# Turning chunks of a ConvFFN's input later and loading operands of its down projection earlier, in a one-layer decoder kernel on one core

## The chip, the core and the metric

The kernel runs on one core of one Trainium2 chip. The metric is device time in microseconds (us). The kernel before took 2790.61 us in the median of three runs (2783.90 to 2791.97); one further execution was profiled.

The engines are named as in the profile: PE is TensorE (matrix products and transposes), DVE is VectorE, ACT is ScalarE, POOL is GpSimd. SP is the engine from which nearly all DMA transfers of this kernel are issued.

## The reference

One layer of a decoder, for a prompt of 2048 tokens (with 16 meta tokens in front) and for 8 sequences that each get one new token over 4096 cached ones. Token mixing is half stick-breaking attention, half pooling over trailing windows. What matters here is the channel mixer behind it, a gated feed-forward with a causal depthwise convolution of width 3:

```python
def conv_ffn(h, prefix, w_up, conv_w, conv_b, w_down):
    up = h @ w_up
    L = up.shape[1]
    ext = jnp.concatenate([prefix.astype(up.dtype), up], axis=1)
    c = conv_b + sum(conv_w[i] * ext[:, i:i + L] for i in range(CONV_W))
    gate, val = c[..., :D_FF], c[..., D_FF:]
    out = (jax.nn.silu(gate) * val) @ w_down
    return out, ext[:, L + 2 - (CONV_W - 1):]
...
        h2 = rmsnorm(xp, norm_ffn_g)
        f, conv_prompt = conv_ffn(h2, zero_prefix, w_up, conv_w, conv_b, w_down)
        xp = xp + f
    y_prompt = rmsnorm(xp, norm_final_g)[:, N_META:]
```

D_MODEL is 1024 and D_FF 2816, so w_up is 1024 x 5632 and w_down 2816 x 1024. All data is float32.

## The kernel before

**Products.** Every float32 operand is split into a high part (a cast to fp32r, on ACT, line 159) and a low part (the difference, on DVE, line 160). A product is three matmuls (lines 165 to 167): high by high, high by low, low by high. The matmuls of 128 x 128 by 128 x 512 accumulate in a PSUM tile of 128 x 512, one bank.

**Stages.** The projection of the input, attention and the mixer's output come first. This document is about the two stages that follow.

The **up projection** runs over 2048 tokens in four chunks of 512 columns (`h2c`, CW = 512) and over 22 pairs of weight tiles (gate and value, NF = 22), in 44 steps `it` (line 998). The steps 0 to 21 take chunks 0 and 1, the steps 22 to 43 take chunks 2 and 3, with all weights loaded a second time. A step loads the next pair of weight tiles (`load_up`, tiles `uwr`, `uwh`, `uwl`, pool `puw` with three buffers of each), and then, for each of its two chunks and for gate and value, makes 24 matmuls into one bank (`psu`), evicts them with the convolution on ACT and DVE (lines 1032 to 1042, tile `cv`), multiplies on POOL and stores the result to `act_s` in DRAM (line 1048).

A chunk stands in DRAM as rows (`h2_s`) and has to be turned: four tiles of 128 rows are loaded (`xn`), each is transposed on PE in two halves of four 128 x 128 blocks (`tp` for chunks 0 and 1, line 794; `tp3c` for chunks 2 and 3, line 821), and each half is split into its place in `h2c`. These halves use the same six PSUM banks as the products (`psu`, pool `pu_mm`). Chunks 0 and 1 are turned by `h2_first` before the first product; the `xn` tiles of `h2_first` borrow buffers of `uwr`, `uwh` and `uwl`. Chunk 2 is turned at the head of steps 4 and 5, two tiles (16 transposes) each; chunk 3 is turned after the last product of step 21, four tiles in a row. It takes the place of chunk 0 (pool `pha`), chunk 2 has a third place (`phb`). Tiles for chunks 2 and 3 have two buffers, so the third tile is loaded when the first is turned (line 823).

Within the up projection the decode of the 8 sequences runs beside the products: gathers on POOL, sums on DVE (lines 876 and 878), values on PE (`dav`, line 946). It ends in step 42, where its memory is released (`dec.close()`, line 1005).

The **down projection** runs over 16 tiles of 128 rows, twice: half `hf` 0 takes the first 11 of the 22 tiles of w_down and adds to the residual, half 1 takes the other 11 and normalises. For a row tile `load_act` loads `ar` (704 KB) and splits it into `ah` and `al`; two halves of 512 columns are then accumulated in `psd`, 33 matmuls each. At the end of the up projection the kernel has loaded the operand of row tile 0 (in step 42, pool `pdx`) and w_down tiles 0 to 2 (in step 43, pool `puw`). Tiles 3 to 10 are loaded at the head of the stage (tile `wd`, pool `pdw`, ten buffers); all pass through the three `uwr` buffers. Row tiles alternate between the pools `pdx` and `pd`, one operand each.

Beside this, ten "few" rows (8 samples and 2 prompt rows) go through the output projection, the up and the down projection in small products (`fewd`, `few`) whose weights come in as `raw` tiles of 512 KB, four buffers. `FSTEP` sets how many of their 42 steps have been emitted before a row tile. The first four `raw` loads, `gfin` (the last gain) and the residual rows `xs` are emitted at the head of the stage, and `conv_states` before row tile 3.

**What sets the order.** The program's order is not the order of each engine: a scheduler that simulates a timeline at build time reorders the instructions within what dependencies and buffers allow. The order on each engine, SP's queue among them, is then fixed in the program.

Of the kernel before, what the change touches and what calls it, by code (L numbers as in the profile page):

```python
# [1 line left out]

# [6 lines left out]
F32 = mybir.dt.float32  # L9
# [9 lines left out]
P = 128  # L19
D = 1024  # L20
NK = D // P
# [23 lines left out]
RAWB = 4  # L45
FSTEP = lambda i: 3 * i // 2
# [14 lines left out]
def hymba_kernel(  # L61
# [710 lines left out]

    def load_act(pool, hf, a0, n):
        ar = pool.tile([P, HF, P], F32, name="ar", bufs=1)
        nc.sync.dma_start(out=ar[:, :, :n], in_=act_s[hf * HF:(hf + 1) * HF, :, a0:a0 + n].rearrange("f p n -> p f n"))
        ah = pool.tile([P, HF, P], F32R, name="ah", bufs=1)
        al = pool.tile([P, HF, P], F32R, name="al", bufs=1)
        split(ah[:, :, :n], al[:, :, :n], ar[:, :, :n])
        return ah, al

    with ExitStack() as es:
        phb = es.enter_context(tc.tile_pool(name="h2b", bufs=2, reuse_waits="tile"))

        def h2_first(ch):

            h2c[ch] = (phb if ch else pha).tile([P, 2, NK, CW], F32R, name="h2c")
            for a in range(4):
                i = 1 + 4 * ch + a
                xn = puw.tile([P, NK, P], F32, name="xn0", tag=("uwr", "uwh", "uwl")[(a + ch) % 3]).rearrange("p c n -> p (c n)")
# [11 lines left out]
        h2_first(1)  # L801
# [11 lines left out]
        def h2_turn(ch, a):  # L813

            if a == 0:
                h2c[ch] = (pha if ch == 3 else phb).tile([P, 2, NK, CW], F32R, name="h2c")
            xn = h2x.pop((ch, a))
            for c4 in range(0, NK, 4):
                tp = psm.tile([P, 4, P], F32, name="tp3c", tag="psu")
                for c in range(4):  # L820
                    nc.tensor.transpose(tp[:, c, :], xn[:, (c4 + c) * P:(c4 + c + 1) * P], ident)
                split(h2c[ch][:, 0, c4:c4 + 4, a * P:(a + 1) * P], h2c[ch][:, 1, c4:c4 + 4, a * P:(a + 1) * P], tp)
            if a < 2:
                h2_load(ch, a + 2)
# [173 lines left out]
        for it in range(2 * NF):  # L998
            half, f = divmod(it, NF)
            ws = ws_next  # L1000
            if it + 1 < 2 * NF:
                ws_next = [load_up((it + 1) % NF), load_up(NF + (it + 1) % NF)]
            if it == 2 * NF - 2:
# [15 lines left out]
            for k in (2 * half, 2 * half + 1):  # L1019
                if 2 * it + k % 2 == 2:  # L1020
# [28 lines left out]
            if it == NF - 1:  # L1049
                for a in range(4):  # L1050
                    h2_turn(3, a)
# [4 lines left out]
    with ExitStack() as es:  # L1056
        pdw = es.enter_context(tc.tile_pool(name="pdw", bufs=HF - 1, side="right", reuse_waits="tile"))
# [20 lines left out]
        nc.sync.dma_start(out=gfin, in_=norm_final_g.partition_broadcast(P))  # L1078
# [91 lines left out]
        nc.sync.dma_start(out=xs[0:NS, :], in_=x_sample)  # L1170
        nc.sync.dma_start(out=xs[NS:NSO, :], in_=meta_tokens[META - 2:META, :])
# [9 lines left out]

        for t in range(RAWB):
            load_raw(t)
        raw_at[0] = RAWB
        dt_ = [(P * i, P, NS + META + P * i) for i in range(16)]
        for hf in range(2):
            wd = []
            for c in range(HF):
                f = hf * HF + c
                if f < 3:  # L1190
                    wd.append(wd_first[c])
                else:
                    wd.append(load_down(f, puw if hf == 1 and 2 <= c < 5 else pdw))
            for ti, (a0, n, xc) in enumerate(dt_):
                if (hf, ti) == (0, 3):
                    conv_states()
                few_to(FSTEP(16 * hf + ti))
                ah, al = act_first if (hf, ti) == (0, 0) else load_act((pdx, pd)[(hf * len(dt_) + ti) % 2], hf, a0, n)
# [40 lines left out]
```

## Time and profile before

| | |
|---|---|
| median of three runs | 2790.61 us (2783.90 to 2791.97) |
| the profiled execution, its own time | 2794.02 us |
| its span, first to last instruction | 2792.3 us |
| mean granted TensorE clock | 0.984 |
| first product of the up projection | 1174.68 us after the start of the span |
| first product of the down projection | 2238.59 us |
| last product of the down projection | 2782.48 us |

How to read the lines in the prediction. A row of the waits has the engine and line that waited, what ended the wait, and then the total in us, the number of times and the longest. A row of the timeline has its start, its length in us, the engine, the line and operation, output and inputs, and in brackets the idle time of the engine ahead of it and what ended that. A row of the stretches has its bounds, its length, the busy time of PE with the number of matmuls (or of all five engines, PE, its weight loads, DVE, ACT and POOL), the granted clock, the share of the DMA engines and GB/s. A row of groups has the line, engine, operation, count, then busy time in total and the mean of one in ns; a row of one tile has the least, median and largest duration in ns. Matmuls overlap: one is shown with 0.39 us, but the next starts 0.23 us after it.

### The profile page before, as it was taken

What the parts mean: (1) busy time and instruction counts of PE and PEld (TensorE: products, weight loads), DVE (VectorE), ACT (ScalarE), POOL (GpSimd) and SP (SyncE); (2) the same over time, 40 slices, a digit from 0 to 9 for tenths busy, and PEclk for the clock granted to TensorE, in tenths of its full rate; (3) what the DMA queues carried; (4) which work ended last, traced back from release to release, by engine and by line L of the source; (5) the groups of instructions that cost most, each with busy time, mean ns of one, the idle gap of its engine ahead of it and who ended that gap; (6) DMA issues with size and microseconds to landing.
All of it is one profiled execution on the core that took longest, in us unless ns stands there. A gap on an engine that the chain in (4) does not pass through costs nothing.

```text
span 2792.3 us, 39757 instructions
## 1 busy us (share of the span) xinstructions
PE 2670.0 (96%) x14759; PEld 2097.0 (75%) x14759; DVE 1805.2 (65%) x3037; ACT 1034.1 (37%) x1833; POOL 718.9 (26%) x736
## 2 busy tenths in 40 slices
PE   5899999999998999899999999999999989999998
PEld 4677877777786888687877777777776767777777
DVE  4588768866769688668977776877774442114434
ACT  4466656655556356323322222222222221002111
POOL 0012112211122011135555554545553200000000
PEclk9899999999999999999999999999999999999999
DMA  7653542464426432545556555646656484666551
GB/s 249 220 186 104 188 162 90 130 212 135 158 91 190 148 109 96 185 162 189 167 207 246 209 199 212 216 177 234 205 216 238 138 282 151 207 202 216 178 177 64
DMA packets 326376, 498.79 MB, mean 179 GB/s; under 512 B 25368, under 2 KB 238632, under 8 KB 309782
## 3 DMA queue, kind: packets, MB, share of 16 engines
q1 hardware_dynamic: 307749, 362.03, 39.5%
q0 software_dynamic: 18432, 134.23, 12.6%
q8 instruction: 116, 1.90, 0.3%
q14 instruction: 79, 0.64, 0.1%
HBM read 395.99 MB, written 100.59 MB: 178 GB/s over the span
## 4 chain that ended last, share of the span: by engine, by line
PE 78%; DVE 3%; DMA 3%; issue 2%; ACT 1%; POOL 0%; SPq 0%; DVEq 0%; ACTq 0%; POOLq 0%
PE psu L165 11%; PE psu L166 11%; PE psu L167 11%; PE psd L165 6%; PE psd L167 5%; PE psd L166 5%; PE po L614 4%; PE z L517 3%; PE tt L571 3%; PE psm L165 2%; PE psm L167 2%; PE psm L166 2%; PE dav L946 2%; PE pso L165 2%; PE pso L167 2%; PE pso L166 2%
## 5 line engine op out<-in xcount | busy, mean ns | idle before, releaser
L165 PE MATMUL psu<-h2c,uwh 128*128 128x512 f32 x1408 | 554.0, 393 | 4.9 <-DVE h2c L160 4.9
L166 PE MATMUL psu<-h2c,uwh 128*128 128x512 f32 x1408 | 551.2, 391 | 0.0
L167 PE MATMUL psu<-h2c,uwl 128*128 128x512 f32 x1408 | 550.3, 391 | 0.0
L533 POOL TENSOR_TENSOR be<-be,om 128x512 f32<-128x512 f32 (+3 forms) x176 | 184.0, 1045 | 841.1 <-DVE om L528 273.8
L1035 DVE SCALAR_TENSOR_TENSOR cv<-psu,par,cv 128x511 f32<-128x511 f32 x352 | 261.2, 742 | 163.8 <-ACT cv L1032 162.1
L165 PEld LDWEIGHTS psu<-h2c,uwh 128*128 128x128 f32 x1408 | 265.3, 188 | 81.2 <-issue 10.3
L1046 POOL TENSOR_TENSOR cv<-cv,cv 128x512 f32<-128x512 f32 x88 | 216.7, 2462 | 373.4 <-DVE cv L1040 285.7
L166 PEld LDWEIGHTS psu<-h2c,uwh 128*128 128x128 f32 x1408 | 265.2, 188 | 62.2 <-issue 8.5
L167 PEld LDWEIGHTS psu<-h2c,uwl 128*128 128x128 f32 x1408 | 265.0, 188 | 61.9 <-issue 7.3
L528 DVE TENSOR_TENSOR_SCAN om<-om,zero 128x513 f32<-128x513 f32 (+1 forms) x224 | 273.2, 1223 | 45.0 <-ACT om L518 40.0
L518 ACT ACTIVATE om<-z,nbias 128x512 f32<-128x512 f32 (+5 forms) x360 | 213.7, 595 | 137.3 <-PE z L517 85.7
L1032 ACT ACTIVATE cv<-psu,par 128x512 f32<-128x512 f32 x176 | 136.6, 776 | 298.2 <-PE psu L167 298.2
L1206 DVE TENSOR_TENSOR xt<-psd,xt 128x512 f32<-128x512 f32 x64 | 44.0, 691 | 285.3 <-PE psd L167 280.5
L519 ACT ACTIVATE be<-z,bias 128x512 f32<-128x512 f32 (+5 forms) x360 | 211.8, 591 | 0.6 <-PE tt L571 0.6
L166 PE MATMUL psm<-hk,wh 128*128 128x512 f32 x512 | 207.4, 405 | 2.9 <-DVE hk L225 2.9
L165 PE MATMUL psm<-hk,wh 128*128 128x512 f32 x512 | 205.9, 408 | 2.0 <-ACT hk L224 1.7
L167 PE MATMUL psm<-hk,wl 128*128 128x512 f32 x512 | 205.3, 401 | 1.1 <-DVE wl L160 1.0
L166 PE MATMUL psd<-wd,ah 128*128 128x512 f32 x512 | 200.8, 393 | 2.9 <-DVE wd L160 2.9
L160 DVE TENSOR_TENSOR uwl<-uwr,uwh 128x1024 fp32r<-128x1024 f32 x94 | 123.5, 1316 | 122.1 <-ACT uwh L159 118.7
L165 PE MATMUL psd<-wd,ah 128*128 128x512 f32 x512 | 201.5, 398 | 0.8 <-ACT wd L159 0.8
L167 PE MATMUL psd<-wd,al 128*128 128x512 f32 x512 | 201.2, 394 | 0.0
L159 ACT CAST uwh<-uwr 128x1024 fp32r<-128x1024 f32 x94 | 98.8, 1053 | 236.7 <-PE psu L166 224.9
(245 smaller groups left out, 4782.9 us busy)
## 6 DMA issues: line engine op xcount, KB each, us to landing
hk<-hs_s SPq DMA_DIRECT2D x96, 512.0 KB
uwr<-in_w_up_dram SPq DMA_DIRECT2D x88, 512.0 KB
act_s<-sg SPq DMA_DIRECT2D x88, 256.0 KB
ar<-act_s SPq DMA_DIRECT2D x32, 704.0 KB
raw<-in_w_up_dram SPq DMA_DIRECT2D x40, 512.0 KB
xt<-in_x_prompt_dram SPq DMA_DIRECT2D x32, 512.0 KB
hs_s<-hk SPq DMA_DIRECT2D x32, 512.0 KB
uwr<-in_w_down_dram SPq DMA_DIRECT2D x22, 512.0 KB
```

Of the source, the lines that this page charges most:

```text
L160: nc.vector.tensor_tensor(out=lo, in0=src, in1=f32(hi), op=ALU.subtract)
L165: nc.tensor.matmul(ps, ah, bh, start=i == 0, stop=False)
L166: nc.tensor.matmul(ps, ah, bl, start=False, stop=False)
L167: nc.tensor.matmul(ps, al, bh, start=False, stop=i == n - 1)
L518: nc.scalar.activation(out=om[:M, e, 0:n], in_=z[:M, :n], func=AF.Sigmoid, scale=-SCALE, bias=nbias[:M, h:h + 1])
L519: nc.scalar.activation(out=be[:M, e, 0:n], in_=z[:M, :n], func=AF.Sigmoid, scale=SCALE, bias=bias[:M, h:h + 1])
L528: nc.vector.tensor_tensor_scan(out=rv, data0=rv, data1=zero[:M, 0:1].broadcast_to([M, n + 1]), initial=st["prev"][:M, e, 0:1], op0=ALU.mul ...
L533: (nc.gpsimd if cnt["mul"] % 2 == 0 else nc.vector).tensor_tensor(out=be[:M, e, m0:n], in0=be[:M, e, m0:n], in1=om[:M, e, m0 + 1:n + 1], o ...
L614: mm = nc.tensor.matmul(o, v_, a_, start=start, stop=stop, skip_group_check=True).ins
L1032: nc.scalar.activation(out=t, in_=ps, func=AF.Identity, scale=cpar(2, fi), bias=cpar(3, fi))
L1035: nc.vector.scalar_tensor_tensor(out=t[:, o:], in0=ps[:, 0:CW - o], scalar=cpar(d, fi), in1=t[:, o:], op0=ALU.mult, op1=ALU.add)
L1046: nc.gpsimd.tensor_tensor(out=cv[1], in0=cv[0], in1=cv[1], op=ALU.mult)
```

## The change

- `h2_first(1)`, the turn of chunk 1, moves from before the first product to step 0, between its products on chunk 0 and those on chunk 1. The load of the weights for step 1 moves behind it. The tiles of chunk 1 borrow other buffers.
- `h2_turn` now turns half a tile. For chunk 2 one half tile is turned before each of the eight chunk passes of steps 4 to 7. For chunk 3 all eight half tiles are turned in step 21 before its pass over chunk 1, as soon as chunk 0 has been used for the last time.
- In step 42 three w_down tiles (3 to 5) are loaded into a new pool `pde` of three buffers; in step 43 the operand of row tile 1 is loaded as well. `load_act` now has two sets of buffers in `pdx`, used in turn for all row tiles. `pdw` has seven buffers, and tiles 5 to 7 of half 1 take those of `pde`.
- The first loads for the few rows move from the head of the stage to row tile 1, `gfin` to row tile 3, and the few rows' steps one row tile later (`FSTEP`).

```diff
-FSTEP = lambda i: 3 * i // 2
+RAWB, WDE = 4, 3
+FSTEP = lambda i: 3 * max(i - 1, 0) // 2
...
     def load_act(pool, hf, a0, n):
-        ar = pool.tile([P, HF, P], F32, name="ar", bufs=1)
+        i = next(act_no) % 2
+        ar = pool.tile([P, HF, P], F32, name=f"ar{i}", bufs=1)
...
         h2_first(0)
         ws_first = [load_up(0), load_up(NF)]
-        h2_first(1)
...
-            if it + 1 < 2 * NF:
+            if 0 < it < 2 * NF - 1:
                 ws_next = [load_up((it + 1) % NF), load_up(NF + (it + 1) % NF)]
             if it == 2 * NF - 2:
...
-                act_first = load_act(pdx, 0, 0, P)
+                pde = ctx.enter_context(tc.tile_pool(name="pde", bufs=WDE, side="right", reuse_waits="tile"))
+                act_first = [load_act(pdx, 0, 0, P)]
+                wd_early = [load_down(3 + c, pde) for c in range(WDE)]
             if it == 2 * NF - 1:
                 wd_first = [load_down(c, puw) for c in range(3)]
+                act_first.append(load_act(pdx, 0, P, P))
...
-            if it in (4, 5):
-                h2_turn(2, 2 * it - 8)
-                h2_turn(2, 2 * it - 7)
...
             for k in (2 * half, 2 * half + 1):
+                if (it, k) == (0, 1):
+                    h2_first(1)
+                    ws_next = [load_up(1), load_up(NF + 1)]
+                if 4 <= it < 8:
+                    h2_turn(2, it - 4, 4 * k)
+                if (it, k) == (NF - 1, 1):
+                    for a in range(4):
+                        for c4 in (0, 4):
+                            h2_turn(3, a, c4)
...
-            if it == NF - 1:
-                for a in range(4):
-                    h2_turn(3, a)
...
-        pdw = es.enter_context(tc.tile_pool(name="pdw", bufs=HF - 1, side="right", reuse_waits="tile"))
+        pdw = es.enter_context(tc.tile_pool(name="pdw", bufs=HF - 1 - WDE, side="right", reuse_waits="tile"))
...
             for ti, (a0, n, xc) in enumerate(dt_):
+                if (hf, ti) == (0, 1):
+                    few_begin()
                 if (hf, ti) == (0, 3):
                     conv_states()
+                    nc.sync.dma_start(out=gfin, in_=norm_final_g.partition_broadcast(P))
```

Where instructions now stand, at three places. First DVE at the start of the up projection, behind the split of the second weight tile and the clearing of `zdec`: `h2c<-tp` are the low parts of chunk 1's half tiles, `cv` the evictions of products, `uwl` a weight tile. Before:

```order
L976 MEMSET zdec 128x2048
L853 TENSOR_SCALAR seg<-seg 128x8
L160 TENSOR_TENSOR h2c<-tp_12760,h2c 128x4x128
L160 TENSOR_TENSOR h2c<-tp_12767,h2c 128x4x128
L931 TENSOR_REDUCE rsel<-hsel 128x4
L933 TENSOR_REDUCE msel<-hsel 128x8
L160 TENSOR_TENSOR h2c<-tp_12776,h2c 128x4x128
L160 TENSOR_TENSOR h2c<-tp_12783,h2c 128x4x128
```

and in the change:

```order
L1048 SCALAR_TENSOR_TENSOR cv_12865<-psu,par,cv_12865 128x511
L161 TENSOR_TENSOR h2c<-tp_12878,h2c 128x4x128
L161 TENSOR_TENSOR h2c<-tp_12885,h2c 128x4x128
L1048 SCALAR_TENSOR_TENSOR cv_12865<-psu,par,cv_12865 128x510
L1055 COPY carry<-psu 128x2
L161 TENSOR_TENSOR uwl<-uwr,uwh 128x1024
L161 TENSOR_TENSOR h2c<-tp_12894,h2c 128x4x128
L858 TENSOR_SCALAR pt_12764<-pt_12764 128x8
L161 TENSOR_TENSOR h2c<-tp_12901,h2c 128x4x128
L161 TENSOR_TENSOR h2c<-tp_12910,h2c 128x4x128
L161 TENSOR_TENSOR h2c<-tp_12917,h2c 128x4x128
```

The half tiles of chunk 1 stood ahead of every eviction and now stand among those of the value product on chunk 0, with a weight tile between them.

Second PE at the turn of chunk 3: `tp3c` are the transposes of a tile, `dav` a step of the decode, `psu` the products. Before:

```order
L821 MATMUL tp3c<-ident,xn_16408 128x128 x8
L821 MATMUL tp3c<-ident,xn_16410 128x128 x8
L946 MATMUL dav<-kvd,zdec 32x512 x8
L821 MATMUL tp3c<-ident,xn_16577 128x128 x8
L821 MATMUL tp3c<-ident,xn_16593 128x128 x8
L165 MATMUL psu<-h2c,uwh 128x512
```

and in the change:

```order
L823 MATMUL tp3c<-ident,xn_16408 128x128 x8
L823 MATMUL tp3c<-ident,xn_16410 128x128 x8
L950 MATMUL dav<-kvd,zdec 32x512 x8
L823 MATMUL tp3c<-ident,xn_16504 128x128 x8
L823 MATMUL tp3c<-ident,xn_16520 128x128 x8
L166 MATMUL psu<-h2c,uwh 128x512
```

The group has moved by 48 matmuls as a whole, and nothing stands between its tiles that did not before.

Third SP's queue at the head of the down projection, from the first of the row tiles' residual loads (`xt`): `uwr` is a tile of w_down, `raw` a tile for the few rows. Before:

```order
L757 DMA uwr<-in_w_down_dram 128x1024
L1078 DMA gfin<-in_norm_final_g_dram 128x1024
L1200 DMA xt_20450<-xp_s 128x1024
L775 DMA ar<-act_s 128x11x128
L1200 DMA xt_20538<-xp_s 128x1024
L1200 DMA xt_20633<-xp_s 128x1024
L757 DMA uwr<-in_w_down_dram 128x1024
L1113 DMA gf<-in_norm_ffn_g_dram 10x1024
L1092 DMA raw<-wf_s 128x1024 x4
```

and in the change:

```order
L1101 DMA raw<-in_w_out_dram 128x1024 x2
L1214 DMA xt_20531<-xp_s 128x1024
L1214 DMA xt_20619<-xp_s 128x1024
L1210 DMA gfin<-in_norm_final_g_dram 128x1024
L1122 DMA gf<-in_norm_ffn_g_dram 10x1024
L1061 DMA act_s<-sg 128x512
L1101 DMA raw<-wf_s 128x1024 x3
L758 DMA uwr<-in_w_down_dram 128x1024
L1077 DMA out_dram<-co 88x128
L1101 DMA raw<-wf_s 128x1024
L758 DMA uwr<-in_w_down_dram 128x1024 x2
```

The operand `ar` is no longer there (four of them now stand further ahead), the loads of `w_out` for the few rows have come in, and the `uwr` loads of w_down tiles 9 and 10 stand behind and between those of `wf_s`.

More of the change, by code (lines that the diff above doesn't have):

```diff
@@ L1 @@
 from contextlib import ExitStack
+from itertools import count
 import concourse.bass as bass
@@ L788, in h2_first @@
                 i = 1 + 4 * ch + a
-                xn = puw.tile([P, NK, P], F32, name="xn0", tag=("uwr", "uwh", "uwl")[(a + ch) % 3]).rearrange("p c n -> p (c n)")
+                xn = puw.tile([P, NK, P], F32, name="xn0", tag=(("uwr", "uwh", "uwl", "uwr"), ("uwh", "uwl", "uwr", "uwr"))[ch][a]).rearrange("p c n -> p (c n)")
                 nc.sync.dma_start(out=xn, in_=h2_s[TILES[i][0]:TILES[i][0] + P, :])
```

47 lines of the change are left out of this document (24 added, 23 removed).

## The prediction

> **What bounds the kernel now.** I read the page first.
>
> ```profile
> PE 2670.0 (96%) x14759; PEld 2097.0 (75%) x14759; DVE 1805.2 (65%) x3037; ACT 1034.1 (37%) x1833; POOL 718.9 (26%) x736
> ```
>
> TensorE (PE) is busy for 2670.0 of the 2792.3 us of the span. Whatever is gained must come out of its idle time, or out of time in which it runs at a lower clock. So the next view is the waits of PE, of which these six rows lie where the change acts (us in total, times, longest):
>
> ```profile
> PE tp L794 <- DMA xn<-h_s: 12.6, 2, 10.6
> PE psu L165 <- DVE h2c L160: 4.9, 1, 4.9
> PE psd L165 <- ACT ah L159: 3.9, 1, 3.9
> PE tp3c L821 <- DMA xn<-h_s: 3.0, 2, 2.7
> PE psd L166 <- DVE wd L160: 2.9, 1, 2.9
> PE fewd L1102 <- DMA raw<-wf_s: 0.5, 2, 0.3
> ```
>
> They are four places: the turn of chunk 1 (tp), that of chunk 2 (psu behind h2c), that of chunk 3 (tp3c), and the start of the down projection (psd, fewd). The third view is the table by stretches for PE alone: length, PE busy (matmuls), granted clock, DMA share, GB/s.
>
> ```profile
> 1156.20:1174.60 18.40, 5.80 (x32) 0.69 0.77 239
> 1174.60:1176.93 2.33, 2.33 (x9) 0.51 0.27 72
> 1200.00:1260.00 60.00, 60.00 (x266) 1.00 0.35 119
> 1293.18:1296.34 3.16, 3.15 (x7) 0.50 1.04 432
> 1704.46:1705.90 1.44, 1.44 (x6) 0.50 0.96 406
> 2249.03:2252.13 3.10, 3.09 (x7) 0.51 1.02 377
> 2263.03:2269.15 6.12, 6.11 (x14) 0.50 0.85 298
> ```
>
> In the undisturbed stretch 266 matmuls take 60.00 us, 0.226 us each. Behind each wait the clock is at half for 1.44 to 6.12 us, which costs half of that time again: a wait costs more than its idle time. Between 1200 and 2240 us PE has no other gaps of size, so a microsecond won at one of these places is won at the end.
>
> **Chunk 1 behind the first products.** The timeline around the start of the up projection:
>
> ```profile
> 1154.83 1.40 PE L794 MATMUL tp<-ident,xn 128*128 128x128 f32 x8 [1.00 <-DVE h2c L160]
> 1159.28 1.21 DVE L160 TENSOR_TENSOR uwl<-uwr,uwh 128x1024 fp32r<-128x1024 f32 x1
> 1160.94 1.05 SPq L790 DMA_DIRECT2D xn<-h_s  x2
> 1162.58 1.23 DVE L160 TENSOR_TENSOR uwl<-uwr,uwh 128x1024 fp32r<-128x1024 f32 x1
> 1166.81 4.42 PE L794 MATMUL tp<-ident,xn 128*128 128x128 f32 x24 [10.58 <-DMA xn<-h_s]
> 1173.26 1.77 PE L794 MATMUL tp<-ident,xn 128*128 128x128 f32 x8 [2.02 <-DMA xn<-h_s]
> ```
>
> Chunk 0 is turned at 1156.2 us and the first weight tile is split at 1160.5 (1159.28 + 1.21), the second at 1163.8. PE nevertheless waits for the loads of chunk 1 and starts its products at 1174.6. The 96 products of the first step (48 for each of two chunks) last 96 x 0.226 = 21.7 us, plus 1.2 us for the half clock: they end at 1197.5.
>
> In the change the 48 products on chunk 0 come first. They start at 1160.5 and take 10.8 us; PE has then been idle for some 4 us, so I add a cooling of 1.5 us as in the rows of 3.10 and 3.16 us. They end at T = 1172.8. The loads of chunk 1 stand in SP's queue where they stood, and the first three of them had landed by 1168 even now, so they are hidden by these products. What comes next is the eviction of the turned pieces. VectorE (DVE) now has them between the evictions of the first products, and PE's second 48 products need seven of the eight pieces:
>
> ```profile
> L160 DVE TENSOR_TENSOR h2c<-tp,h2c x16: 675/681/692, 1154.0 to 1175.7; 128x512 fp32r<-128x512 f32 x16
> L1035 DVE SCALAR_TENSOR_TENSOR cv<-psu,par,cv 128x511 f32<-128x511 f32 x352 | 261.2, 742 | 163.8 <-ACT cv L1032 162.1
> L1032 ACT ACTIVATE cv<-psu,par 128x512 f32<-128x512 f32 x176 | 136.6, 776 | 298.2 <-PE psu L167 298.2
> L160 DVE TENSOR_TENSOR uwl<-uwr,uwh 128x1024 fp32r<-128x1024 f32 x94 | 123.5, 1316 | 122.1 <-ACT uwh L159 118.7
> ```
>
> After T: 0.78 (ScalarE's cv) + 2 x 0.74 + 7 x 0.68 + 1.32 (one weight tile) = 8.3 us, with the small copies 8.7. The second 48 products start at 1181.5 and, with 10.8 us and 1.2 us of half clock, end at 1193.5. **Gain 4.0 us**, much less than the 12.6 us of waiting, since the eviction of the pieces becomes the wait. Ends: 0.5 us if both coolings last 6.12 us, 7 us if neither occurs.
>
> [...]
>
> **Chunk 2 in half tiles.** Today four half tiles are turned at a time:
>
> ```profile
> 1286.38 1.91 PE L821 MATMUL tp3c<-ident,xn 128*128 128x128 f32 x16
> 1287.56 2.27 DVE L878 TENSOR_REDUCE zdec<-kvd 128x32 f32<-128x2048 f32 x1
> 1293.19 0.80 PE L165 MATMUL psu<-h2c,uwh 128*128 128x512 f32 x1 [4.90 <-DVE h2c L160]
> ```
>
> The second such block fills four of six PSUM banks while DVE is busy with the decode, and PE waits 4.9 us for a bank, then 3.16 us at half clock (1.6 us lost). One piece at a time takes one bank, before each of eight pairs of product groups; five banks are left for products that last 24 x 0.226 = 5.4 us each. The 32 transposes and 16 evictions stay. **Gain 6.5 us**; at worst the waits come back in small pieces and only the 1.6 us of clock remain, above 6.5 there is nothing to win.
>
> **Chunk 3** is moved half a step earlier, but its four tiles are still turned in a row.
>
> ```profile
> 1701.48 1.06 PE L821 MATMUL tp3c<-ident,xn 128*128 128x128 f32 x8 [2.67 <-DMA xn<-h_s]
> ```
>
> Its third tile is loaded into the buffer of its first one, so the load still starts with the turn, and PE's order there is the same (two tiles, a decode step, two tiles). **Gain 0**; ends -2 (a load later) and +3.7 (3.0 us of wait and 0.7 of clock).
>
> **Start of the down projection.** What is lost there now: 3.9 + 2.9 + 0.5 us idle, and half of 3.10 and 6.12 us, together 11.9 us. The rows from which the new course is worked out:
>
> ```profile
> 2224.70 4.50 SPq L1092 DMA_DIRECT2D raw<-in_w_out_dram  x4
> 2238.59 0.40 PE L165 MATMUL psd<-uwh,ah 128*128 128x512 f32 x1
> 2243.66 4.32 SPq L1092 DMA_DIRECT2D raw<-wf_s  x4
> 2247.62 1.36 ACT L159 CAST ah<-ar 128x1408 fp32r<-128x1408 f32 x1 [7.33 <-DMA ar<-act_s]
> 2257.94 1.03 PE L1102 MATMUL fewd<-raw,catsm 128*10 128x512 f32 x4 [0.32 <-DMA raw<-wf_s]
> L159 ACT CAST wd<-uwr x16: 1039/1048/1053, 2248.9 to 2539.4; 128x1024 fp32r<-128x1024 f32 x16
> L160 DVE TENSOR_TENSOR wd<-uwr,wd x16: 1201/1218/1228, 2261.8 to 2540.5; 128x1024 fp32r<-128x1024 f32 x16
> uwr<-in_w_down_dram SPq DMA_DIRECT2D x22, 512.0 KB
> 2240.00:2250.00 10.00, 6.07 (x32) 3.28 (x31) 3.88 (x8) 2.67 (x4) 2.57 (x2) 0.93 0.97 331
> 2250.00:2260.00 10.00, 9.45 (x37) 4.52 (x35) 1.59 (x3) 1.93 (x2) 0.00 (x0) 0.90 1.06 377
> ```
>
> With two row tiles and six weight tiles ready, PE has 2 x 2 x 6 x 3 = 72 products, 16.2 us, in the times of before from 2238.6 to 2254.8. The early splits (three more wd and one ah: 3 x 1.05 + 1.36 on ScalarE) fall where the decode has ended and neither engine is full, and their loads come before the queue fills: nothing. In exchange the four w_out rows of the few, which land under the up projection today, land after it; from their place in SP's queue they have until 2254.8, which is enough. Their eight products (1 us, they exist today too) release the buffers for wf_s. Only then, at about 2256, does SP issue three wf_s loads, weight tile 9, a wf_s load and weight tile 10: 6 x 512 KB = 3.1 MB, 8.3 to 9.5 us at the 377 to 331 GB/s that these stretches show. Tile 10 has landed at some 2265 and is split 1.05 + 1.22 us later, at 2267; tile 9 at 2265. PE has 36 products of tiles 6 to 8 until then (8.1 us, to 2264.5) and 2.7 us for tile 9: about 0.5 us of waiting. Row tiles 2 and 3 can only be split when 0 and 1 are done, as they end together: 1.4 us of cast. With one short cooling I put the new loss at 2.9 us. **Gain 9.0 us.** Ends: 11.9 with no loss; 3 if tiles 9 and 10 take as long as the wf_s rows did today, 10 us from the last issue at 2248 to the use at 2257.94 (5 us idle, 3.1 of clock, the cast).
>
> The later steps of the few rows and the loads of gfin and the states move behind other tiles and stay off the end: the last few product comes two row tiles before the last one, 30 us ahead.
>
> **Sum:** 4.0 + 6.5 + 0 + 9.0 = 19.5 us. The profiled execution took 2794.0 us, so 2774.5; it lies 3.4 us above the median of the three runs, 2790.6, against which I forecast **2771 us**.
>
> **Rivals.** A change under 0.3% (8.4 us) cannot be told from none.
>
> Late transfers. Tiles 9 and 10 and the few rows' loads arrive one behind the other, and PE, which takes its order as written, waits and cools each time. For it speaks the DMA share of 0.97 to 1.06 in those stretches, against it the three weight tiles that are no longer in them. The down projection then gives 3: 13.5 us in all, 2777; with the small end of chunk 1 as well, 10 us, 2780.6, and worse where it happens at each row tile change.
>
> Evictions in the way. The pieces, now between the evictions, hold up the products: chunk 1 gives 0.5 and chunk 2 only 1.6: 11.1 us, 2779.5; together with a down projection at 3 it is 5.1 us, no change. For it speaks DVE, which takes 2.27 us at a time for the decode; against it the free banks.
>
> Warm start. The first products, and perhaps those after the turn, run at full clock, as the row of 1200 us shows it: without the 1.5 and the 1.2 us chunk 1 gives 5.5 to 6.7, 2769. The half clock behind each of the four waits speaks against it. [...]
>
> Slower: ScalarE held by the early weights. The first early split writes room that the decode leaves, and stands in ScalarE's order ahead of the cast of the last up tile.
>
> ```profile
> 2207.29 0.26 DVE L970 COPY catsm<-sot 128x16 f32<-128x16 f32 x2
> 2211.37 1.06 ACT L159 CAST uwh<-uwr 128x1024 fp32r<-128x1024 f32 x1 [3.80 <-PE psu L166]
> ```
>
> The decode ends at 2207.3; two wd casts and one ah cast, 3.5 us, end at 2210.8, in time for the cast at 2211.4. Its group of products starts 72 x 0.226 = 16.3 us before 2238.6, at 2222.3, and the split with what now stands ahead of it on DVE takes some 6 us (1.06 + 2 x 1.22 + 1.6 + 1.2): 5 us of slack. From there each microsecond by which the decode ends later is one of PE; slower than before by 0.3% needs 33 us of delay in all, and gives about 2799. The decode's gathers do start later, since their indices come behind the pieces, but by less than 10 us, and 40 steps lie between.
>
> **Chances.** Forecast 0.60; warm start 0.06; late transfers 0.20 (half of it still faster by over 8.4 us, 0.01 slower); evictions 0.10 (0.06 faster); ScalarE held 0.04 (slower). That makes faster 0.82, same 0.13, slower 0.05. The terms' ends sum to 3 us and 29 us (2787.5 and 2761.5); the range that leaves out 2 in 10 is 2764 to 2785.
>
> **What would show it.** In the profile after: the first psu product near 1160 and a wait of PE for DVE's h2c of 3 to 6 us near 1178 in place of the 10.6; no wait of psu for h2c near 1290; the tp3c wait still there; no wait for ah near 2249, and none above 2 us before the first wd product that follows. The forecast is wrong if these waits are gone and the span isn't 12 us or more shorter, or if PE waits over 5 us in all for raw, wd or ah within 40 us of the first psd.

## The result, and the profile after

| | before | after |
|---|---|---|
| median of the runs on one chip | 2791.29 us (2783.90 to 2794.77, four runs) | 2771.26 us (2766.84 to 2774.24, four runs) |
| the profiled execution | 2794.02 us | 2771.54 us |
| its span | 2792.3 us | 2769.8 us |
| mean granted TensorE clock | 0.984 | 0.988 |

The ratio after/before is 0.9931, with a 95% interval of 0.9915 to 0.9946: 19 us faster (15 to 24). The two profiled executions differ by 22.5 us, since that of before was 2.7 us above its median.

The page of after, busy time of the engines:

```profile
PE 2662.7 (96%) x14759; PEld 2089.6 (75%) x14759; DVE 1805.2 (65%) x3037; ACT 1031.4 (37%) x1833; POOL 721.7 (26%) x736
```

PE makes the same 14759 matmuls in 7.3 us less: the time at half clock has shrunk, from 30.71 to 10.24 us in the four sections below. The rest of the 22.5 us is idle time. The waits of PE in after, at the same places as those shown of before (total in us, times, longest):

```profile
PE psu L166 <- ACT uwh L160: 2.2, 1, 2.2
PE tp3c L823 <- DMA xn<-h_s: 1.9, 2, 1.0
PE psd L166 <- ACT ah L160: 1.4, 2, 1.1
PE psu L166 <- ACT h2c L160: 1.4, 1, 1.4
PE psu L168 <- DVE uwl L161: 1.3, 1, 1.3
PE psd L168 <- DVE ms L141: 0.6, 1, 0.6
PE psu L166 <- DVE h2c L161: 0.3, 1, 0.3
```

The waits of 12.6 (tp for xn), 4.9 (psu for h2c), 2.9 (psd for wd) and 0.5 us (fewd for raw) are gone, and that of 3.9 us (psd for ah) is 1.4 us now. In their place stand 5.2 us around the first products (uwh, uwl, h2c). The wait for chunk 3's third and fourth tile is still there, 1.9 us.

The timeline around the first products of after:

```profile
1152.34 2.78 PE L798 MATMUL tp<-ident,xn 128*128 128x128 f32 x24
1159.71 0.49 PE L166 MATMUL psu<-h2c,uwh 128*128 128x512 f32 x1 [2.18 <-ACT uwh L160]
1173.77 3.67 PE L798 MATMUL tp<-ident,xn 128*128 128x128 f32 x28
1179.66 0.49 PE L166 MATMUL psu<-h2c,uwh 128*128 128x512 f32 x1 [1.44 <-ACT h2c L160]
1180.48 1.00 PE L166 MATMUL psu<-h2c,uwh 128*128 128x512 f32 x2 [0.32 <-DVE h2c L161]
```

The stage begins 1.3 us later than in before (1152.34 against 1151.05, in code that is the same). Counted from there, the first product comes at 1158.4 of before's time and the second turn at 1172.5. Behind the first product PE waits another 1.29 us for the low part of the weights (uwl). The evictions of chunk 1's pieces stop PE for only 1.44 and 0.32 us.

PE at the start of the down projection in after (two of the five groups of the few rows' products there, and all waits):

```profile
2243.71 1.05 PE L1111 MATMUL fewd<-raw,catsm 128*10 128x512 f32 x8
2252.52 1.03 PE L1111 MATMUL fewd<-raw,catsm 128*10 128x512 f32 x4
2263.76 0.50 PE L166 MATMUL psd<-uwh,ah 128*128 128x512 f32 x1 [0.33 <-ACT ah L160]
2266.07 0.50 PE L166 MATMUL psd<-uwh,ah 128*128 128x512 f32 x1 [1.11 <-ACT ah L160]
2267.91 0.50 PE L168 MATMUL psd<-uwh,al 128*128 128x512 f32 x1 [0.65 <-DVE ms L141]
```

**Where the time went, by sections.** Six moments cut the up and the down projection into pieces that hold at most one part of the change each: the first transposition (tp), the 8th, the 44th and the 169th copy of `carry` from psu (steps 1, 10 and 42 in DVE's order), and the first and the last product of the down projection (psd). The first three sections and the last one hold parts A (chunk 1 behind the first products), B (chunk 2 in half tiles), C (chunk 3) and D (start of the down projection). The piece between C and D, up to the first psd, lasts 36.5 us in every profile and is left out. Read from the timelines, with the time at half clock within each section in brackets, in us:

| kernel | A | B | C | D |
|---|---|---|---|---|
| before | 72.16 (13.65) | 209.39 (3.41) | 769.48 (3.41) | 543.89 (10.24) |
| after | 66.49 (6.83) | 202.93 (0) | 768.69 (3.41) | 533.05 (0) |
| difference | 5.7 | 6.5 | 0.8 | 10.8 |

They sum to 23.8 us; less the 1.3 us by which the stage starts later, that is the 22.5 us of the two spans.

### The profile page after: what moved, and what is told of

The parts are those of the page before. It is cut to its first block, busy times and chain, and to the rows that moved or that the text cites. A ratio compares the mean times of both kernels' runs of the same rounds, so it can differ in the third digit from the quotient of the medians.

```text
span 2769.8 us, 39760 instructions
## 1 busy us (share of the span) xinstructions
PE 2662.7 (96%) x14759; PEld 2089.6 (75%) x14759; DVE 1805.2 (65%) x3037; ACT 1031.4 (37%) x1833; POOL 721.7 (26%) x736
## 4 chain that ended last, share of the span: by engine, by line
PE 79%; DVE 3%; issue 2%; DMA 2%; ACT 1%; POOL 0%; SPq 0%; DVEq 0%; ACTq 0%; POOLq 0%
PE psu L166 12%; PE psu L167 12%; PE psu L168 12%; PE psd L166 6%; PE psd L168 6%; PE psd L167 6%; PE po L615 4%; PE z L518 3%; PE tt L572 3%; PE dav L950 2%; PE psm L166 2%; PE psm L168 2%; PE psm L167 2%; PE pso L167 2%; PE pso L166 2%; PE pso L168 2%
## 5 line engine op out<-in xcount | busy, mean ns | idle before, releaser
L166 PE MATMUL psu<-h2c,uwh 128*128 128x512 f32 x1408 | 555.0, 394 | 4.0 <-ACT uwh L160 2.2
L167 PE MATMUL psu<-h2c,uwh 128*128 128x512 f32 x1408 | 551.6, 392 | 0.0
L166 PEld LDWEIGHTS psu<-h2c,uwh 128*128 128x128 f32 x1408 | 265.2, 188 | 81.1 <-issue 10.9
L1059 POOL TENSOR_TENSOR cv<-cv,cv 128x512 f32<-128x512 f32 x88 | 224.7, 2554 | 388.6 <-DVE cv L1053 290.7
L167 PEld LDWEIGHTS psu<-h2c,uwh 128*128 128x128 f32 x1408 | 265.3, 188 | 62.1 <-issue 8.5
L167 PE MATMUL psm<-hk,wh 128*128 128x512 f32 x512 | 206.6, 404 | 2.9 <-DVE hk L226 2.9
L166 PE MATMUL psm<-hk,wh 128*128 128x512 f32 x512 | 205.0, 406 | 1.9 <-ACT hk L225 1.3
L166 PE MATMUL psd<-wd,ah 128*128 128x512 f32 x512 | 200.3, 395 | 0.0
L167 PE MATMUL psd<-wd,ah 128*128 128x512 f32 x512 | 200.0, 392 | 0.0
```

The lines of the kernel that those rows point to most:

```text
L166: nc.tensor.matmul(ps, ah, bh, start=i == 0, stop=False)
L167: nc.tensor.matmul(ps, ah, bl, start=False, stop=False)
L1059: nc.gpsimd.tensor_tensor(out=cv[1], in0=cv[0], in1=cv[1], op=ALU.mult)
```

## The experiments

All are compared with the kernel before, run on the same chip at the same time. Their profiles fill the table of sections further on. The last eight kernels start from the changed one, but were run apart from it, and their intervals all overlap that of the change (0.9915 to 0.9946). Their medians alone therefore do not tell them from the changed kernel; what is said of a difference to it rests on the sections of one profile each.

**One part alone (four kernels).** Each applies one part of the diff to the kernel before.

```diff
 a_alone: h2_first(1) and the load for step 1 within step 0, before chunk 1's products
 b_alone: h2_turn in half tiles, h2_turn(2, it - 4, 4 * k) in steps 4 to 7
 c_alone: h2_turn(3, ...) in step 21 before k = 1
 d_alone: pde, the second act_first, few_begin, FSTEP, gfin, load_act in two sets
```

> Only the turn of chunk 1 is moved (first part of the change), all else as before. Theory of the forecast: the gain of a part is what its own place on PE gives, so 4.0 us by the forecast's sum; by the trace of the changed kernel it should be 5.7 us (its second step of the up projection begins 4.4 us earlier, though the stage itself starts 1.3 us later there). Rival 'not on the path': later waits swallow it and the gain is under 1 us.

> Only chunk 2 is turned in half tiles, all else as before. Theory: 6.5 us faster (4.9 us of waiting for a bank and 1.6 us of half clock), no wait of psu for h2c near 1290. Rival 'evictions in the way': 1.6 us, with small waits before several groups.

> Only chunk 3 is turned before the second chunk pass of step 21 instead of behind it, four tiles in a row as before. Theory: no gain (-0.5 to 1 us), and PE still waits 2 to 3 us for the load of the third tile. Rival 'the earlier start hides the load': 2.5 to 3.7 us faster and no such wait.

> Only the start of the down projection is changed (second operand and three weight tiles early, few rows' loads later), the up projection is as before. Theory: 9.0 us by the forecast's sum, 10.8 us by the trace of the changed kernel, with some 2 us of waits for ah. Rival 'late transfers': 3 us, with waits of over 5 us for weight tiles 9 and 10 or raw tiles. If the four parts are independent, the four gains add up to the whole change's 20 to 22.5 us.

| | median | ratio to before, 95% interval |
|---|---|---|
| before | 2790.83 us | |
| a_alone | 2785.61 us | 0.9985 (0.9976 to 0.9994) |
| b_alone | 2782.61 us | 0.9973 (0.9963 to 0.9983) |
| c_alone | 2789.84 us | 0.9996 (0.9987 to 1.0005) |
| d_alone | 2779.80 us | 0.9965 (0.9952 to 0.9979) |

By the ratios the parts give 4.2, 7.5, 1.1 and 9.8 us, together 22.6 us; the whole change gave 19 us (15 to 24). They add up within their uncertainty, and each is near its term of the sum. The rivals "not on the path" (a_alone), "evictions in the way" (b_alone) and "late transfers" (d_alone) fall: their 1, 1.6 and 3 us lie outside the intervals. In b_alone no wait of psu for h2c is left and the half tiles follow one another as in after, at equal distances and without a wait:

```profile
1258.46 0.60 PE L823 MATMUL tp3c<-ident,xn 128*128 128x128 f32 x4
1269.81 0.60 PE L823 MATMUL tp3c<-ident,xn 128*128 128x128 f32 x4
```

For c_alone neither theory can be told from no change by the time alone; its waits of tp3c for xn are 1.9 us in place of 3.0.

**The down projection taken apart (three kernels, from the changed one).** few_at_head gives the few rows their old place, no_early_wd loads w_down tiles 3 to 5 at the head of the stage, op1_pd takes the second row tile's operand from the pool that opens with the stage.

```diff
 few_at_head
-                if (hf, ti) == (0, 1):
-                    few_begin()
+        few_begin()          (at the head of the stage, gfin too, FSTEP as before)
 no_early_wd
-                wd_early = [load_down(3 + c, pde) for c in range(WDE)]
 op1_pd
-                act_first.append(load_act(pdx, 0, P, P))
-                ah, al = act_first[ti] if hf == 0 and ti < 2 else load_act(pdx, hf, a0, n)
+                ah, al = act_first[0] if (hf, ti) == (0, 0) else load_act((pdx, pd)[(hf * len(dt_) + ti) % 2], hf, a0, n)
```

> The changed kernel, but the first loads of the few rows, gfin and the few rows' steps stand where they stood before the change (head of the down projection). Theory: the second operand and the early weight tiles bring the gain of this part, the delay of the few rows little: 18 to 20 us faster than before (2771 to 2773), PE waits for raw or wd below 2 us in all. Rival 'late transfers': without the delay the few rows' loads stand ahead of weight tiles 6 to 10, PE waits over 3 us for them, 16 us faster than before or less (2775 or more).

> The changed kernel, but w_down tiles 3 to 5 are loaded at the head of the down projection as before the change; the second operand is early and the few rows are late as in the change. Theory: the wait for the first of these tiles (2.9 us before the change) and the half clock behind it come back, at least 6 us slower than the changed kernel (2777 or more). Rival: the few rows' delay alone frees the queue, and the tiles land in time: 2771 to 2773.

> The changed kernel, but the second row tile's operand comes from the pool that opens with the down projection, as before the change, not from the second set that is there in the last step of the up projection. Theory: the wait for ah behind the first row tile (3.9 us before the change) and one half-clock stretch (1.7 us) come back: 4 to 6 us slower than the changed kernel. Rival: the three early weight tiles and the late few rows are what counts, 0 to 1 us slower.

few_at_head took 2773.01 us in the median, ratio 0.9937 (0.9924 to 0.9951), as the theory had it: the delay of the few rows brings little, 2.2 us by section D. PE waits there once, for the operand:

```profile
2267.52 0.50 PE L168 MATMUL psd<-uwh,al 128*128 128x512 f32 x1 [2.16 <-DVE al L161]
```

But PE is idle for 2.1 us in section D of after as well. The 2.2 us are busy time of PE, as the stretches of section D show, in after, few_at_head and op1_pd (length, PE busy with the number of matmuls, granted clock, DMA share, GB/s):

```profile
2226.97:2760.02 533.05, 530.96 (x2636) 1.00 0.56 189
2223.60:2758.89 535.29, 533.13 (x2636) 1.00 0.57 188
2222.83:2752.51 529.68, 529.04 (x2636) 1.00 0.57 189
```

The matmuls are the same in number. few_at_head makes its first few products in runs of 8, 4 and 2 instead of 8 and 4, and a run of 2 holds up the next matmul as long as one of 8 does in after (0.96 and 0.98 us from start to start). A run of 2 in few_at_head, with what follows:

```profile
2253.30 1.03 PE L1112 MATMUL fewd<-raw,catsm 128*10 128x512 f32 x2
2254.26 1.20 PE L166 MATMUL psd<-wd,ah 128*128 128x512 f32 x4
```

no_early_wd took 2775.69 us, 0.9946 (0.9933 to 0.9960), 4.4 us above after's median where 6 was the least expected; section D is 7.3 us longer than in after (3.4 us of it idle time of PE), so the early weight tiles carry most of part D. But the wait is another than the theory named. The scheduler, which has 36 products ready and not 72, puts the few rows' products behind these 36, and PE waits there for raw tiles; then the clock is at half for 6.83 us (from 2240.11):

```profile
2233.29 1.03 PE L1109 MATMUL fewd<-raw,catsm 128*10 128x512 f32 x4 [0.86 <-DMA raw<-in_w_out_dram]
2241.14 1.89 PE L1109 MATMUL fewd<-raw,catsm 128*10 128x512 f32 x4 [4.38 <-DMA raw<-wf_s]
```

op1_pd was a miss: 2764.81 us, ratio 0.9907 (0.9891 to 0.9924), not slower than the changed kernel at all; its section D is 3.4 us shorter (529.68 us), where seven profiles of the change lie between 533.05 and 533.70 us. Its edit also brings back the two pools in turn for the later row tiles. Before the change the second operand was cast at 2247.62, 9.0 us after the first psd, and PE stood still for 3.93 us. In op1_pd ACT casts it 6.4 us after the first psd at 2222.83, and PE does not wait for it:

```profile
2225.72 1.91 PE L1109 MATMUL fewd<-raw,catsm 128*10 128x512 f32 x16
2241.72 1.90 PE L1109 MATMUL fewd<-raw,catsm 128*10 128x512 f32 x16
```

```profile
2229.23 1.38 ACT L160 CAST ah<-ar 128x1408 fp32r<-128x1408 f32 x1 [4.70 <-DMA ar<-act_s]
```

With six weight tiles instead of three, row tile 0 alone has 2 x 6 x 3 = 36 products (8.1 us) and not 18 to run while that operand lands. So the wait for ah was also a matter of too few weight tiles. And as its row tiles come one after the other, their operands are split one after the other too: of the waits after 2263, 2.1 us of idle time, 0.6 us are left. The other 1.9 us is PE busy time (529.04 against 530.96 us). op1_pd makes its few products in runs of 16 rather than 4 and 8, and few_at_head, with runs down to 2, is off to the other side; so the length of the runs may be the reason, but no run changed it alone.

**The first products.** fill adds transposes that nobody reads, turn_mid moves the turn of chunk 1:

```diff
 fill (in h2_first, behind the last tile of chunk 0)
+            if ch == 0:
+                fl = pst.tile([P, 4, P], F32, name="fill", tag="tp3")
+                for c in range(24):
+                    nc.tensor.transpose(fl[:, c % 4, :], xn[:, (4 + c % 4) * P:(5 + c % 4) * P], ident)
 turn_mid (in the loop over gate and value, s)
+                    if (it, k, s) == (0, 0, 1):
+                        h2_first(1)
```

> The changed kernel with 24 further transposes of the last tile of chunk 0 into a bank that nobody reads, between the turn of chunk 0 and the first product (3.2 us of PE work in the gap of 2.2 and 1.3 us). Theory: the half clock follows PE's idle time, so the half clock from 1162 to 1165 goes and the kernel is 1 to 1.5 us faster than the changed one. Rival: the half clock belongs to the change of work and stays, or the filler itself delays the products: 0 to 1 us slower.

> The changed kernel, but chunk 1 is turned in the middle of chunk 0's 48 products (between gate and value, 24 each) instead of behind them. Theory: the evictions of the pieces are then covered by 24 products, the waits of psu for h2c (1.4 and 0.3 us) and the half clock behind them (1.6 us) go: 3 us faster than the changed kernel. Rival: the tiles of chunk 1, issued at 1157.6 to 1162.7, have not landed 5.4 us earlier; PE waits 2 us or more for xn and nothing is won.

fill took 2764.85 us, 0.9906 (0.9892 to 0.9919). Section A is 3.0 us shorter than in after and has no half clock at all, with 24 transposes more in it. In fill and combo, which have the filler, section A has no half clock; in the eight other profiles with chunk 1 turned later it has 6.83 or 10.24 us. So the half clock there went with idle PE, and here the filler was cheaper than the gap. The 1.43 us wait for h2c behind the second turn is the same as in after, and there too the clock stayed at 1.00, which the theory had not said. By the author's estimate that is not the filler's work but a matter of how the gap lay (see the last section): PE is idle for 1.45 and 0.57 us of two stretches of 3.41 us there (from 1172.56 and 1175.97, both at 1.00), and in after for 1.62 us of a single one (from 1178.40), with 3.41 us at half behind it. The median lies 6.4 us below after's. Of the 6.1 us between the two profiled executions, 3.0 us are this section, 0.9 us section C, which has no stretch at half clock in fill, and 2.1 us the stage ahead, whose code is the same.

turn_mid took 2766.16 us, 0.9908 (0.9893 to 0.9923). PE in turn_mid:

```profile
1157.98 0.49 PE L166 MATMUL psu<-h2c,uwh 128*128 128x512 f32 x1 [2.18 <-ACT uwh L160]
1168.03 4.47 PE L798 MATMUL tp<-ident,xn 128*128 128x128 f32 x32
```

The tiles of chunk 1 have landed by 1168, and nothing waits behind the turn but one product for 0.5 us: section A is 63.94 us, 2.5 us less than after, near the 3 us expected. The waits went as the theory said, the half clock did not: it is 6.83 us in both profiles, all of it behind the first products in turn_mid. The idle time of PE in section A is 1.8 us less (4.83 against 6.64 us).

**Chunk 3 in two parts, and combinations.** c3_split turns two tiles of chunk 3 before the second chunk pass of step 21 and two before the first pass of step 22. mid_c3 is c3_split and turn_mid, combo has the filler of fill too.

```diff
-                if (it, k) == (NF - 1, 1):
-                    for a in range(4):
+                if (it, k) in ((NF - 1, 1), (NF, 2)):
+                    for a in (0, 1) if k == 1 else (2, 3):
```

> The changed kernel, but of chunk 3 two tiles are turned before the second chunk pass of step 21 and two behind it, so that 48 products (10.8 us) lie between the first tile's turn, which starts the load of the third, and the third's. Theory: the waits of tp3c for xn (1.9 us) and the half clock behind them (1.7 us) go, 1.9 to 3.6 us faster than the changed kernel. Rival: the second pair now waits for the load or its eviction in turn, no gain.

> The changed kernel with chunk 1 turned in the middle of chunk 0's products and chunk 3 in two parts. Theory: both add up, 5 to 6 us faster than the changed kernel (2765 to 2766). Rival: one of them takes back the other, 3 us or less.

> The same with the 24 filler transposes ahead of the first product as well. Theory: the half clock behind the first products goes too (3.4 or 6.8 us at half, so 1.7 or 3.4 us): 7 to 9 us faster than the changed kernel (2762 to 2764). Rival: without a low half of the weights the filler only moves the wait, no faster than without it.

c3_split took 2765.73 us, 0.9907 (0.9891 to 0.9924). The loads that had kept PE waiting are now covered by the 48 products between the two turns:

```profile
1671.53 1.91 PE L823 MATMUL tp3c<-ident,xn 128*128 128x128 f32 x16
1684.19 1.91 PE L823 MATMUL tp3c<-ident,xn 128*128 128x128 f32 x16
```

Section C is 765.04 us, with no idle time of PE at all, 3.7 us less than after and 2.8 us less than the mean of the change (below). mid_c3 took 2764.44 us, 0.9901 (0.9884 to 0.9917): 6.8 us below after's median, and sections A and C are as short as in the kernels with one of the edits (64.00 and 765.04 us), so both add up. Its median is the lowest here, but op1_pd, fill, combo, c3_split and turn_mid lie within 1.8 us of it and can't be told from it by time; op1_pd's edit was not combined with the others. combo took 2765.08 us, 0.9906 (0.9889 to 0.9922), no faster than mid_c3, as its rival said but for another reason. The filler took the half clock away, and PE came to the turn before the tiles had landed:

```profile
1170.70 1.06 PE L798 MATMUL tp<-ident,xn 128*128 128x128 f32 x8 [2.92 <-DMA xn<-h_s]
```

**The sections of all profiles** (us, time at half clock in brackets; "first tp" is the start of section A):

| kernel | first tp | A | B | C | D |
|---|---|---|---|---|---|
| a_alone | 1148.81 | 67.54 (10.24) | 209.97 (6.83) | 769.47 (3.41) | 541.93 (6.83) |
| b_alone | 1150.01 | 72.10 (13.65) | 202.96 (0) | 769.40 (3.41) | 540.07 (6.83) |
| c_alone | 1151.49 | 70.00 (13.65) | 210.72 (6.83) | 767.73 (0) | 543.12 (13.65) |
| d_alone | 1150.19 | 69.94 (10.24) | 210.35 (6.83) | 768.26 (0) | 533.05 (0) |
| few_at_head | 1150.90 | 65.53 (6.83) | 202.93 (0) | 767.73 (0) | 535.30 (0) |
| no_early_wd | 1149.17 | 66.44 (6.83) | 202.93 (0) | 767.73 (0) | 540.38 (6.83) |
| fill | 1150.23 | 63.49 (0) | 202.93 (0) | 767.75 (0) | 533.05 (0) |
| turn_mid | 1150.61 | 63.94 (6.83) | 202.93 (0) | 767.72 (0) | 533.06 (0) |
| c3_split | 1151.37 | 65.69 (6.83) | 202.96 (0) | 765.04 (0) | 533.22 (0) |
| op1_pd | 1147.99 | 67.63 (10.24) | 202.93 (0) | 767.77 (0) | 529.68 (0) |
| mid_c3 | 1152.21 | 64.00 (6.83) | 202.93 (0) | 765.04 (0) | 533.70 (0) |
| combo | 1152.99 | 63.87 (0) | 202.93 (0) | 765.04 (0) | 533.14 (0) |

Where a section's code is that of before, four profiles each give means of 71.05, 210.11, 769.15 and 542.25 us. Where it is that of the change (six, ten, seven and seven profiles) they are 66.55, 202.94, 767.88 and 533.18 us. So the parts are worth 4.5, 7.2, 1.3 and 9.1 us, together 22.0 us.

## Why the prediction was right

The forecast of 2771 us, a gain of 19.5 us taken from the median of 2790.6, met the median of 2771.26 us. That the numbers meet so closely is luck. The terms were 4.0, 6.5, 0 and 9.0 us and the means of the sections 4.5, 7.2, 1.3 and 9.1 us. In the two profiled executions, and the forecast was worked out from that of before, the sections gained 5.7, 6.5, 0.8 and 10.8 us, 23.8 us in all. The scatter of single executions (2766.84 to 2774.24 us) is larger than these differences. What the runs bear out is the four places and the rough size of each.

**Chunk 1 (forecast 4.0, measured 4.5): right in size, wrong in a step.** The second turn came when the working said (1172.5 against 1172.8, in before's time); the first product came 2.1 us sooner (1158.4 against 1160.5), and the wait for uwl and the half clock took most of that back. The step that failed is "the eviction of the pieces becomes the wait", with PE's second 48 products behind seven of the eight pieces and a wait of 3 to 6 us. PE waited 1.8 us. The working took it that the products on chunk 1 come next. The scheduler puts products of step 1 on chunk 0 there, whose weights are ready, as PE's order in the changed program shows (the PSUM tile of a product, the chunk it reads, and the number of its matmuls in a row):

```
psu_12810 h2c_12678 x24
psu_12840 h2c_12678 x24
(32 transposes of chunk 1)
psu_12952 h2c_12875 x1
psu_12984 h2c_12875 x1
psu_13039 h2c_12678 x23
psu_12952 h2c_12875 x23
```

Here h2c_12678 is chunk 0 and h2c_12875 chunk 1. PE's rows in after have the same pattern: three matmuls of L166 in a row at 1179.66 and 1180.48, and two of L167 in a row where the products on chunk 1 go on:

```profile
1187.73 0.62 PE L167 MATMUL psu<-h2c,uwh 128*128 128x512 f32 x2
1179.66 3.07 DVE L161 TENSOR_TENSOR h2c<-tp,h2c 128x512 fp32r<-128x512 f32 x5
```

Two matmuls on chunk 1 stand ahead and make the 1.8 us of waits; then 23 on chunk 0 (5.2 us at full clock) cover the evictions. These took as long as forecast: DVE ends the last one at 1182.73, 9.0 us after the second turn began, against 8.7. The cost was right, and that PE has to wait for it was wrong. What was saved there was in part lost to the clock: the forecast had 1.5 and 1.2 us of cooling, the six profiles with this order have 6.83 or 10.24 us at half clock, 3.4 or 5.1 us lost if all of it fell on work. So the two errors nearly cancel, and that the size came out right is luck. fill, without any, gives 63.49 us, a gain of 7.6 us on the mean of before: the forecast's end "neither occurs", 7 us, was about right.

**Chunk 2 (6.5, measured 7.2): right.** Section B is 202.93 to 202.96 us in ten profiles, with no wait. The 0.7 us above the forecast is before's: its profiled execution had 3.41 us at half clock there, three others 6.83 us, so "above 6.5 there is nothing to win" held for that execution only.

**Chunk 3 (0, measured 1.3): right that the wait stays,** 1.9 us instead of 3.0. A decode step (dav) stands between the second tile and the third in both kernels:

```profile
1675.10 1.98 PE L950 MATMUL dav<-kvd,zdec 128*32 128x512 f32 x16
1678.13 1.06 PE L823 MATMUL tp3c<-ident,xn 128*128 128x128 f32 x8 [1.05 <-DMA xn<-h_s]
```

What differs is the load. From the issue of the third tile's load to its first transpose it is 5.4 us in before and 3.8 us in after (PE alone, as above):

```profile
1696.07:1701.48 5.41, 2.75 (x24) 1.00 0.97 363
1674.33:1678.13 3.80, 2.75 (x24) 1.00 0.61 212
```

PE is busy for 2.75 us in both, while the DMA engines are busy for 0.97 of the time in the first and 0.61 in the second. c_alone, with chunk 3 moved alone, has the same 1.9 us of waits there as after. The working looked at the order and not at what else the DMA engines do at the new place. That their other transfers are the reason is read from these rows; no run changed them alone. Part of the 1.3 us is the clock: three of the four profiles with the old place have 3.41 us at half clock in section C, and of the seven with the new place only after has it.

c3_split shows what the place was worth, 4.1 us against the mean of before and 2.8 us against that of the change: the end that the forecast gave (+3.7) was there to be had by another order.

**Start of the down projection (9.0, measured 9.1): right in the sum, part of the reason wrong.** No wait for tiles 9 and 10 came (0.5 us forecast), the waits ahead of products that read ah and al were 2.1 us (1.4 forecast; 0.65 us of them are put down to ms), and there was no cooling. The rival "late transfers" did not come to pass; even without the delay of the few rows (few_at_head) PE waits for no raw or wd tile, and section D is 2.2 us longer. What the working did not see is that the early operand of the second row tile brings nothing once six weight tiles are there: op1_pd, without it, has the shorter section D.

The rival "warm start" was named with 5.5 to 6.7 us for chunk 1. It did not happen in the profile of after (3.41 us at half from 1161.33), and without filler none of the eight profiles with chunk 1 turned later has less than 6.83 us at half clock in section A.

## What to carry to other kernels

Read the order that the scheduler made before you cost a new wait. At the start of the up projection it filled the hole with other products, and the wait that the program's order suggested did not come; in no_early_wd it filled the hole with the few rows' products, and PE waited for their loads instead. When a stage starts with too few operand tiles, try tiles whose products cover the next load first: here three weight tiles did most of it, and a further early operand brought nothing. And count the half clock behind a gap by an average over several executions, since it differed here from one to the next with the same gap: with the same wait of psu for h2c (4.9 us), section B had 3.41 us of it in before and 6.83 us in a_alone, c_alone and d_alone.

## What the runs showed of the hardware

**The half clock in these profiles.** In the clock records of before and after, the nine stretches at half clock between the first transposition and the last product last 3.41 us (seven of them), 6.83 us or 10.24 us; the sums by section, in the table of all 14 profiles, are 3.41, 6.83, 10.24 or 13.65 us wherever there is any. Their starts lie a multiple of 3.41 us apart within one execution (1161.33, 1181.81 and 1680.15 in after: 6 times and 146 times as much). So the stretches below are cut into steps of 3.41 us. The same waits, 2.18 and 1.29 us, stand ahead of the first products in after and in turn_mid, and 3.41 us at half follow in the one, 6.83 us in the other. Stretches of after by these steps (length, PE busy with the number of matmuls, granted clock, DMA share, GB/s):

```profile
1157.91:1161.33 3.42, 0.85 (x2) 1.00 0.88 258
1161.33:1164.74 3.41, 2.89 (x7) 0.50 0.73 239
1164.74:1168.16 3.42, 3.42 (x17) 1.00 0.90 238
1178.40:1181.81 3.41, 1.79 (x6) 1.00 0.95 298
1181.81:1185.22 3.41, 3.41 (x10) 0.50 1.05 263
```

and of turn_mid:

```profile
1155.83:1159.25 3.42, 0.85 (x2) 1.00 0.97 275
1159.25:1162.66 3.41, 2.54 (x6) 0.50 0.72 228
1162.66:1166.08 3.42, 3.42 (x9) 0.50 0.98 275
1166.08:1169.49 3.41, 3.41 (x23) 1.00 1.04 355
```

In both the step in which PE was idle for 2.57 us is followed by one at half. In after 0.52 us of the second wait fall into that one (PE busy for 2.89 us) and the clock is at 1.00 behind it; in turn_mid 0.87 us do (2.54 us busy), and it is at half for one step more. A wait of 2.7 us for the same load is followed by half clock in b_alone, where 2.72 us of idle time lie within one step, and not in d_alone, where 1.39 and 1.78 us lie in two. First b_alone, then d_alone:

```profile
1690.70:1694.11 3.41, 0.69 (x9) 1.00 0.92 328
1694.11:1697.53 3.42, 3.42 (x17) 0.50 1.09 403
```

```profile
1694.68:1698.09 3.41, 2.02 (x17) 1.00 0.91 344
1698.09:1701.50 3.41, 1.63 (x13) 1.00 1.05 375
1701.50:1704.91 3.41, 3.41 (x19) 1.00 1.01 424
```

So 1.62 us of idle time in a step were followed by half clock at 1178.40 in after, and 1.78 us at 1698.09 in d_alone were not. In combo, PE's wait of 2.92 us ahead of 1170.70 was not followed by half clock either (1.00 from 1166.69 to 1173.52). In the profiles of before and after, between the first transposition and the last product, PE was idle for 1.62 to 3.41 us in the nine steps at full clock with half clock behind them, and for 1.53 us or less in all others at full clock. Of the twelve steps at half clock, nine had full clock behind them, with PE idle for 0.52 us or less, and three had half clock, with 0.73 us (2262.31 in before) and twice 3.41 us (1159.81 and 1163.22 in before). What decides is not shown by these profiles. The prediction counted a cooling behind every such gap; the gaps of d_alone and combo had none.

**The stage ahead scatters by 5 us.** The first transposition comes between 1147.99 and 1152.99 us in 14 executions of code that is the same up to there. The sections beside it, where no half clock falls, agree to 0.03 us (B of the change, 202.93 to 202.96 us in ten profiles). A single profile is therefore read by sections, and not by its end.
